# A one-layer decoder trunk with three branches on one core: key tiles 0 and 1 formed together, warm-up products, split operands for sums over partitions, and another order of work at stage ends and in the last rows

## The chip, the cores and the metric

The kernel runs on one core of a Trainium2 chip. TensorE (PE) multiplies matrices, VectorE (DVE) and ScalarE (ACT) do the element-wise work, GpSimd (POOL) issues the stores and some loads, SyncE (SP) issues most loads. Each engine works through its own row of instructions in a fixed order and waits on semaphores of the others. The metric is the device time of the launch in microseconds (us), the median of several runs.

## The reference

One layer on 1024 tokens of width 1024, with a memory of 256 tokens. The functions are cut to their core:

```python
h = rms_norm(x, norm_g)                       # x / sqrt(mean(x^2) + eps) * g
z = einsum('bsd,de->bse', h, w_in)            # 11 column blocks of 1024
u, v, gate_a = gelu(z_u), layer_norm(gelu(z_v)), silu(z_ga)
br_a = gmlp_spatial_gate(u, v, w_s, b_s) * gate_a          # causal within chunks of 128
c = causal_depthwise_conv(z_ba * sigmoid(z_bb), conv_w, conv_b)   # 31 taps
br_b = silu(layer_norm(c, conv_ln_g, conv_ln_b)) * silu(z_gb)
mem_n = rms_norm(mem, mem_norm_g)
att = memory_cross_attention(z_q, mem_n, w_kv)             # 4 heads of 256
br_c = att * silu(z_gc)
proj = einsum('bsnw,nwd->bsnd', [br_a, br_b, br_c], w_branch)
merged = einsum('bsnd,bsnd->bsd', sigmoid(z_merge), proj)
out = rms_norm(x + einsum('bsd,de->bse', merged, w_out), final_norm_g)
```

## The kernel before

All arrays lie in SBUF tiles of 128 partitions. Each large operand is split into two fp32r parts, hi (a cast on ACT) and lo (the difference, on DVE; `split`, lines 74 and 75), and a product is the sum of three: hi by hi, lo by hi, hi by lo. A product named "128x512" in the trace has 512 columns. Products with fp32 operands that are not split show as two records each.

The program goes through these stages, in PE's order (times from the trace):

- Keys (line 231, from 5.86 us): the transposed memory, scaled by its gain (`mhi`, `mlo`, lines 187 and 188), against eight weight tiles e, 24 products of 256 columns each. The sum of squares of memory (`msum`) is added up by DVE (line 130), summed over partitions on PE with a column of ones (line 109 in `mean_rsqrt`), turned into 1/sqrt, and spread over all partitions (`spread`: diagonal matrices `dg` on DVE, line 120, against `ones` on PE, line 121, copied out by ACT, line 122).
- Values of the memory (line 280, from 35 us), eight weight chunks.
- Branch A's v (line 322, from 56 to 149 us): for each half th of the tokens and each half ch of the columns, four weight chunks c, each 24 products of 512 columns into four banks. The first half uses the raw x times its gain (`xg`), and the norm of x, needed by all that comes later, is formed beside it: squares of the eight tiles of x on ACT, adds into `xsum` on DVE (line 130), column sums on PE (line 109), `spread` into `rb`.
- Pairs (line 365, 149 to 928 us): 40 pairs of column tiles of the other blocks, each formed in seven block products instead of eight; x, y, z are its three banks, `op` are split operands, `s1` to `s4` sums of weight quarters, and `u`, `ca`, `cb` intermediate sums on ACT and DVE.
- Branches (line 622, from 929 us): for each branch n in the order 0, 2, 1 and each column tile d, 48 products into `acc`; attention stands between, and the mean (line 764) and the spread of the conv's layer norm between the tiles of n = 2.
- Output projection (line 841, to 1325 us) and the last rows: residual, mean square, 1/sqrt, scaling, store (lines 857 to 875).

A scheduler places instructions in each engine's row when the program is built, by the dependences and by the slots of the pools: a tile takes a slot of its ring (`op`: 6 slots, `raw`: 3, `dg`: 4 in a pool of its own), and a writer stands behind the readers of the slot's last tenant. `keep` fixes the order of loads on SP. Weight chunks come by `wchunk`, a cast of a whole 128x1024 load and its difference.

Of the kernel before, what the change touches and what calls it, by code (L numbers as in the profile page):

```python
# [39 lines left out]
def trunk(ctx, tc, xt, x, memt, wf, wv, wkf, wkv, wbr, wo, wst, bs, cols, fng, out):  # L40
# [110 lines left out]
    A.dma_start(out=col, in_=cols)  # L151

# [32 lines left out]
    for k in range(KT):  # L185
# [3 lines left out]
                               op0=ALU.mult, op1=ALU.subtract)  # L189
    mrb = const.tile([P, M], F32, name="mrb")  # L190
# [27 lines left out]
    for e in range(KT):  # L218
        kv_ahead(e + NAHEAD)
        x_load(e)  # L220
        if e:
            hi, lo = wchunk(None, ahead[e])
        else:
            hi, lo = op((P, 1024), "whi"), op((P, 1024), "wlo")
            for v in (slice(0, H), slice(H, 2 * H)):
                split(ahead[0][:, v], hi[:, v], lo[:, v])
        ps = bank()
        for k in range(KT):
            ks = slice(k * P, (k + 1) * P)
            for j, (w, m) in enumerate(((hi, mhi), (hi, mlo), (lo, mhi))):  # L230
                T.matmul(ps[:, :M], w[:, ks], m[k], start=(k == 0 and j == 0), stop=(k == KT - 1 and j == 2))  # L231
        late.append((e, ps))
# [313 lines left out]
    for p in range(4):  # L546
        for i, (blk, fn, then) in enumerate((
# [20 lines left out]
            pump(PUMP[i])  # L568

# [1 line left out]
    ready = {}  # L571
    order = [(n, d) for n in (0, 2, 1) for d in range(KT)]
    raws = []

# [421 lines left out]
```

## Time and profile before

| what | value |
|---|---|
| median of three runs | 1333.65 us (1333.63 to 1335.38) |
| profiled execution: span from first to last instruction | 1333.8 us |
| PE busy | 1316.5 us (99%) in 6084 records |
| DVE busy | 1079.5 us (81%) |
| ACT busy | 595.3 us (45%) |
| POOL busy | 61.3 us (5%) |
| bytes moved | 179.99 MB |

A timeline row gives the start, the length, the engine, the line, the operation with out<-in by the program's names, and in brackets the idle time before it with what ended it. Products overlap in the pipeline, so the price of one is the distance to the next one's start, not its length.

### The profile page before, as it was taken

What the parts mean: (1) busy time and instruction counts of PE and PEld (TensorE: products, weight loads), DVE (VectorE), ACT (ScalarE), POOL (GpSimd) and SP (SyncE); (2) the same over time, 40 slices, a digit from 0 to 9 for tenths busy, and PEclk for the clock granted to TensorE, in tenths of its full rate; (3) what the DMA queues carried; (4) which work ended last, traced back from release to release, by engine and by line L of the source; (5) the groups of instructions that cost most, each with busy time, mean ns of one, the idle gap of its engine ahead of it and who ended that gap; (6) DMA issues with size and microseconds to landing.
All of it is one profiled execution on the core that took longest, in us unless ns stands there. A gap on an engine that the chain in (4) does not pass through costs nothing.

```text
span 1333.8 us, 16115 instructions
## 1 busy us (share of the span) xinstructions
PE 1316.5 (99%) x6084; PEld 1098.6 (82%) x6084; DVE 1079.5 (81%) x1438; ACT 595.3 (45%) x967; POOL 61.3 (5%) x120
## 2 busy tenths in 40 slices
PE   8999999999999999999999999999999999999997
PEld 7888888888888888888888888887888888888886
DVE  6799759969966998986996996796797486944797
ACT  6757634334444344434434444345544443502256
POOL 0000000000000000000000000001000010000000
PEclk9999999999999999999999999999999999999999
DMA  9634312342222333223333213338555354633323
GB/s 372 248 110 158 135 62 81 111 142 96 103 78 79 121 118 140 88 79 111 111 110 120 95 48 127 127 111 297 188 181 171 112 190 157 228 119 111 142 96 126
DMA packets 60126, 179.99 MB, mean 135 GB/s; under 512 B 5904, under 2 KB 15248, under 8 KB 60048
## 3 DMA queue, kind: packets, MB, share of 16 engines
q1 hardware_dynamic: 44464, 122.96, 27.2%
q0 software_dynamic: 15296, 55.58, 10.9%
q8 instruction: 47, 0.77, 0.2%
q10 hardware_dynamic: 288, 0.42, 0.1%
q14 instruction: 31, 0.25, 0.1%
HBM read 131.75 MB, written 47.19 MB: 134 GB/s over the span
## 4 chain that ended last, share of the span: by engine, by line
PE 95%; DVE 2%; ACT 1%; issue 0%; DMA 0%; SPq 0%; DVEq 0%; ACTq 0%
PE x L365 33%; PE acc L622 19%; PE y L365 16%; PE z L365 8%; PE b L322 6%; PE acc L841 5%; PE b L231 2%; PE acc L660 2%; PE acc L696 2%; PE b L280 1%; PE sp L534 1%; DMA mraw<-in_memt 0%; DVE xsum L130 0%; PE acc L681 0%; ACT y L874 0%
## 5 line engine op out<-in xcount | busy, mean ns | idle before, releaser
L365 PE MATMUL x<-T,op 128*128 128x512 f32 x1440 | 347.5, 390 | 0.7 <-ACT u L404 0.7
L365 PEld LDWEIGHTS x<-T,op 128*128 128x128 f32 x1440 | 269.8, 188 | 57.4 <-ACT u L404 1.1
L74 ACT CAST op<-sum 128x512 fp32r<-128x512 f32 x160 | 99.5, 622 | 132.2 <-PE z L365 56.4
L456 DVE SCALAR_TENSOR_TENSOR conv<-cb,col,conv 128x994 f32<-128x994 f32 (+14 forms) x120 | 151.8, 1265 | 0.5
L75 DVE TENSOR_TENSOR op<-sum,op 128x512 fp32r<-128x512 f32 x160 | 109.4, 686 | 36.0 <-ACT op L74 35.7
L622 PE MATMUL acc<-bhi,whi 128*128 128x512 f32 x384 | 119.7, 393 | 0.9 <-DVE ca L414 0.9
L622 PE MATMUL acc<-bhi,wlo 128*128 128x512 f32 x384 | 119.1, 390 | 0.0
L622 PE MATMUL acc<-blo,whi 128*128 128x512 f32 x384 | 118.7, 390 | 0.0
L365 PE MATMUL x<-B,op 128*128 128x512 f32 x480 | 115.5, 389 | 0.0
L365 PE MATMUL z<-B,op 128*128 128x512 f32 x480 | 115.3, 389 | 0.0
L365 PE MATMUL y<-T,op 128*128 128x512 f32 x480 | 115.3, 389 | 0.0
L365 PE MATMUL y<-B,op 128*128 128x512 f32 x480 | 115.3, 389 | 0.0
L456 DVE SCALAR_TENSOR_TENSOR conv<-ca,col,conv 128x994 f32<-128x994 f32 (+14 forms) x90 | 113.7, 1263 | 0.2
L74 ACT CAST op<-raw 128x512 fp32r<-128x512 f32 x120 | 74.3, 620 | 79.3 <-PE y L365 77.9
L75 DVE TENSOR_TENSOR op<-raw,op 128x512 fp32r<-128x512 f32 x120 | 82.1, 686 | 33.4 <-ACT op L74 33.4
L365 PEld LDWEIGHTS y<-B,op 128*128 128x128 f32 x480 | 90.1, 188 | 18.7
L365 PEld LDWEIGHTS y<-T,op 128*128 128x128 f32 x480 | 90.1, 188 | 18.7
L365 PEld LDWEIGHTS z<-B,op 128*128 128x128 f32 x480 | 90.1, 188 | 18.7
L365 PEld LDWEIGHTS x<-B,op 128*128 128x128 f32 x480 | 90.1, 188 | 18.7
L622 PEld LDWEIGHTS acc<-blo,whi 128*128 128x128 f32 x384 | 72.1, 188 | 15.5 <-DVE blo L75 0.4
L622 PEld LDWEIGHTS acc<-bhi,wlo 128*128 128x128 f32 x384 | 72.1, 188 | 15.0
L622 PEld LDWEIGHTS acc<-bhi,whi 128*128 128x128 f32 x384 | 71.3, 188 | 15.9 <-issue 1.7
(231 smaller groups left out, 1961.2 us busy)
## 6 DMA issues: line engine op xcount, KB each, us to landing
raw<-in_wf SPq DMA_DIRECT2D x80, 512.0 KB, 3.5
raw<-in_wbr SPq DMA_DIRECT2D x24, 512.0 KB, 4.4
gate<-g SPq DMA_DIRECT2D x24, 512.0 KB, 4.2
raw<-in_wv SPq DMA_DIRECT2D x16, 512.0 KB, 3.6
g<-cb POOLq DMA_DIRECT2D x12, 512.0 KB, 3.1
g<-ca POOLq DMA_DIRECT2D x12, 512.0 KB, 2.9
xr<-in_xt SPq DMA_DIRECT2D x8, 512.0 KB, 10.5
kvraw<-in_wkv SPq DMA_DIRECT2D x8, 512.0 KB, 10.7
```

The costliest lines, as they stand in the source:

```text
L74: A.copy(hi, src)
L75: V.tensor_tensor(lo, src, f(hi), ALU.subtract)
L231: T.matmul(ps[:, :M], w[:, ks], m[k], start=(k == 0 and j == 0), stop=(k == KT - 1 and j == 2))
L280: T.matmul(pst[m], a[k][:, ms], w[:, ws], start=(k == 0 and j == 0), stop=(k == KT - 1 and j == 2))
L322: T.matmul(pst[t], q[:, a, ts_], w[:, ws], start=(k == 0 and j == 0), stop=(k == KT - 1 and j == 2))
L365: T.matmul(ps, w[:, a, ks], m[k][:, b, :], start=(start and k == 0 and j == 0), stop=(stop and k == 3 and j == 2), skip_group_check=not start)
L456: V.scalar_tensor_tensor(out=a[:, PAD - j:], in0=g[:, :n], scalar=col[:, cw + j:cw + j + 1], in1=a[:, PAD - j:], op0=ALU.mult, op1=ALU.add)
L534: T.matmul(ps[:, t * P:(t + 1) * P], va[:, 4 * hf + t, :], ws[:, i, :], start=True, stop=True)
L622: T.matmul(ps[:, hf, :], w[:, ks], m[k][:, hf * H:(hf + 1) * H], start=(k == 0 and j == 0), stop=(k == KT - 1 and j == 2))
L660: T.matmul(ps[:, i, :], q[a][:, d, i * P:(i + 1) * P], kk[:, b, d, :], start=(d == 0 and j == 0), stop=(d == 1 and j == 2))
L696: T.matmul(ps[:, d, :], vv[:, a, m, d * P:(d + 1) * P], p2[b][:, m, :], start=(m == 0 and j == 0), stop=(m == MT - 1 and j == 2))
L841: T.matmul(ps[t], a[k][i][:, ts_], w[k][n], start=(start and k == 0 and j == 0), stop=(k == 3 and j == 2), skip_group_check=not start)
```

## The change

Six parts. (1) Ten products of `ones` by `ones` are issued before the first key product; key tiles 0 and 1 are formed side by side, k by k, and the loads of weights and memory alternate in halves. (2) `spread` splits the factor into `rh` and `rl`, builds up to four diagonal matrices by one DVE instruction in a tile of the `op` ring, and spreads by two products of up to 512 columns with an fp32r matrix of ones. (3) In the last pair, the product into z and the start of the branches (`start_branches`) stand between the os3 product and the last one into x. (4) The conv's mean takes a split `csum` and an fp32r `onesd`. (5) The last row tile of the output is formed in two halves of 256 columns. (6) The final norm's small steps are fewer and placed anew, and its last scaling is cut at column 640 instead of 512.

```diff
+        rh = small.tile([P, n], F32R, tag=f"rh{n}", name=nm("rh"))
+        rl = small.tile([P, n], F32R, tag=f"rl{n}", name=nm("rl"))
+        split(r, rh, rl)
+        groups = []
         for i0 in range(0, n, 4):
             w = min(4, n - i0)
+            dg = wpool.tile([P, 2, 4, P], F32R, tag="op", name=nm("dg"), bufs=NOP)
+            for j, v in enumerate((rh, rl)):
+                V.tensor_tensor(dg[:, j, :w, :], ident[:, None, :].broadcast_to([P, w, P]),
+                                f(v)[:, i0:i0 + w, None].broadcast_to([P, w, P]), ALU.mult)
+            groups.append((i0, w, dg))
+        for i0, w, dg in groups:
             ps = mk()
-            for i in range(w):
-                dg = small.tile([P, P], F32, tag="dg", name=nm("dg"), bufs=4)
-                V.tensor_scalar(dg, ident, r[:, i0 + i:i0 + i + 1], None, ALU.mult)
-                T.matmul(ps[:, i * P:(i + 1) * P], ones, dg, start=True, stop=True)
+            for j in range(2):
+                T.matmul(ps[:, :w * P], onesr, dg[:, j, :w, :].rearrange("p a b -> p (a b)"), start=(j == 0),
+                         stop=(j == 1))
             A.copy(dst[:, i0 * P:(i0 + w) * P], ps[:, :w * P])
...
-    onesd = const.tile([P, P], F32, name="onesd")
-    G.memset(onesd, 1.0 / D)
+    onesd = const.tile([P, P], F32R, name="onesd")
+    onesr = const.tile([P, P], F32R, name="onesr")
...
+    ahead.append(slot(s="kvraw"))
+    keep(nc.sync.dma_start(out=ahead[1][:, :H], in_=wkf[1][:, :H]))
     keep(nc.sync.dma_start(out=mraw[0][:, 2:, :], in_=memt[0][:, 2:, :]))
     keep(nc.sync.dma_start(out=ahead[0][:, H:], in_=wkf[0][:, H:]))
-    keep(nc.sync.dma_start(out=mraw[1], in_=memt[1]))
-    kv_ahead(2)
+    keep(nc.sync.dma_start(out=mraw[1][:, :2, :], in_=memt[1][:, :2, :]))
+    keep(nc.sync.dma_start(out=ahead[1][:, H:], in_=wkf[1][:, H:]))
+    keep(nc.sync.dma_start(out=mraw[1][:, 2:, :], in_=memt[1][:, 2:, :]))
+    warm = bank("warm")
+    for _ in range(NWARM):
+        T.matmul(warm[:, :P], ones, ones, start=True, stop=True)
...
+    first = [(op((P, 1024), "whi"), op((P, 1024), "wlo")) for _ in range(2)]
+    for i in range(2):
+        v = slice(i * H, (i + 1) * H)
+        for e in range(2):
+            split(ahead[e][:, v], first[e][0][:, v], first[e][1][:, v])
+            for k in range(4 * i + 2 * e, 4 * i + 2 * e + 2):
+                mem_gain(k)
...
+        if e != 1:
+            group = [(bank(), *(wchunk(None, ahead[e]) if e else first[0]))]
+            if e == 0:
+                group.append((bank(), *first[1]))
+            for k in range(KT):
+                ks = slice(k * P, (k + 1) * P)
+                for ps, hi, lo in group:
+                    for j, (w, m) in enumerate(((hi, mhi), (hi, mlo), (lo, mhi))):
+                        T.matmul(ps[:, :M], w[:, ks], m[k], start=(k == 0 and j == 0),
+                                 stop=(k == KT - 1 and j == 2))
+            for i, g in enumerate(group):
+                late.append((e + i, g[0]))
...
-        o12 = operand(a12)
+        ca, cb = slot(s="ca"), slot(s="cb")
+
+        def second():
+            o12 = operand(a12)
+            prod(z, o12, B[1][0], True, True)
+            V.tensor_tensor(ca[:, :H], z, p1, ALU.add)
+
         V.tensor_tensor(s3, a11, a21, ALU.subtract)
         V.tensor_tensor(s4, a12, s2, ALU.subtract)
-        prod(z, o12, B[1][0], True, True)
-        ca, cb = slot(s="ca"), slot(s="cb")
-        V.tensor_tensor(ca[:, :H], z, p1, ALU.add)
+        if not between:
+            second()
...
         prod(x, os3, T3, False, True)
         u3 = half("u3")
         A.copy(u3, x)
+        if between:
+            second()
+            between()
         V.tensor_tensor(cb[:, H:], y, u3, ALU.add)
...
+    def start_branches():
+        for e in range(NPRE):
+            branch_tile(e, bra[e])
+        for d in range(NRDY):
+            ready[0, d] = weights(0, d)
...
-            pair(blk, p, kept(fn, then))
+            pair(blk, p, kept(fn, then), start_branches if (p, i) == (3, 9) else None)
...
+    csr = wchunk(None, csum)
...
-                T.matmul(ps[:, hf, :], onesd, csum[:, hf * H:(hf + 1) * H], start=True, stop=True)
+                for j in range(2):
+                    T.matmul(ps[:, hf, :], onesd, csr[j][:, hf * H:(hf + 1) * H], start=(j == 0), stop=(j == 1))
...
+            for v in ((slice(0, M), slice(M, H)) if t == fine else (slice(0, H),)):
+                for k in range(4):
+                    for j, (i, n) in enumerate(((0, 0), (1, 0), (0, 1))):
+                        T.matmul(ps[t][:, v], a[k][i][:, ts_], w[k][n][:, v], start=(start and k == 0 and j == 0),
+                                 stop=(k == 3 and j == 2), skip_group_check=not start)
...
+    def yend(i):
+        m, s, y, t, rr = fa[:, i, 1:2], *[fr[:, i, j:j + 1] for j in range(4)]
+        A.activation(out=s, in_=m, func=AF.Sqrt)
+        V.reciprocal(out=y, in_=s)
+        V.scalar_tensor_tensor(out=t, in0=y, scalar=m, in1=y, op0=ALU.mult, op1=ALU.mult)
+        V.tensor_scalar(t, t, -0.5, 1.5, ALU.mult, ALU.add)
+        V.tensor_tensor(rr, y, t, ALU.mult)
+        rows = slice(i * P, (i + 1) * P)
+        if i == 3:
+            w = 640
+            A.activation(out=ys[i][:, w:], in_=ys[i][:, w:], func=AF.Copy, scale=rr)
+            A.dma_start(out=out[rows, w:], in_=ys[i][:, w:])
+            V.tensor_scalar(ys[i][:, :w], ys[i][:, :w], rr, None, ALU.mult)
+            nc.sync.dma_start(out=out[rows, :w], in_=ys[i][:, :w])
...
-    oprod(py, o, w, False)
-    yadd(0, 1, py, 2)
+    oprod(py, o, w, False, 3)
+    for t in range(3):
+        ypart(t, 1, H, 2 * H, py[t], 2)
+        yend(t)
+    ypart(3, 1, H, H + M, py[3][:, :M], 3)
+    ypart(3, 1, H + M, 2 * H, py[3][:, M:], 2, 1)
+    yend(3)
```

What moves in the engines' rows, at three places. In the names, a number tells tiles of one name apart; `x2` is two equal rows; in brackets stands the semaphore waited for.

PE in the first half of branch A's v, before: the end of the second weight chunk (`wlo_165`), the third (`whi_168`), and the column sums of `xsum`.

```order
L322 MATMUL b_136_682<-wlo_165_787,xg_91_487 128x512
L322 MATMUL b_133_679<-whi_168_820,xg_97_498 128x512 [waits Activation_49]
L322 MATMUL b_133_679<-whi_168_820,xg_97_498 128x512
L322 MATMUL b_134_680<-whi_168_820,xg_97_498 128x512 x2
L322 MATMUL b_133_679<-wlo_169_821,xg_97_498 128x512 [waits DVE_49]
L322 MATMUL b_133_679<-whi_168_820,xg_101_519 128x512 x2
L322 MATMUL b_133_679<-wlo_169_821,xg_101_519 128x512
L322 MATMUL b_134_680<-wlo_169_821,xg_97_498 128x512
L109 MATMUL b_147_735<-ones_72,xsum_9_114 128x1 [waits DVE_49]
L109 MATMUL b_147_735<-ones_72,xsum_9_114 128x1 x7
L322 MATMUL b_134_680<-whi_168_820,xg_101_519 128x512 x2
```

The same engine and stage with the change: `whi_140` and `wlo_141` are the first weight chunk, `whi_162` and `wlo_163` the second, `dg` the diagonal matrices.

```order
L348 MATMUL b_138_702<-whi_140_705,xg_78_425 128x512 x2
L348 MATMUL b_138_702<-wlo_141_706,xg_78_425 128x512
L109 MATMUL b_149_755<-ones_72,xsum_14_141 128x1 [waits DVE_49]
L109 MATMUL b_149_755<-ones_72,xsum_14_141 128x1 x7
L129 MATMUL b_159_786<-dg_157_780,onesr_75 128x512 [waits DVE_49] x2
L129 MATMUL b_160_790<-dg_158_783,onesr_75 128x512 [waits DVE_49,Activation_49]
L348 MATMUL b_135_699<-whi_162_796,xg_86_466 128x512 [waits Activation_49]
L348 MATMUL b_135_699<-whi_162_796,xg_86_466 128x512
L129 MATMUL b_160_790<-dg_158_783,onesr_75 128x512 [waits DVE_49]
L348 MATMUL b_136_700<-whi_162_796,xg_86_466 128x512 x2
L348 MATMUL b_137_701<-whi_162_796,xg_86_466 128x512 x2
L348 MATMUL b_135_699<-wlo_163_797,xg_86_466 128x512 [waits DVE_49]
```

The column sums have moved from behind the second chunk and seven products of the third to the place right behind the first chunk, and the spread stands among the first products of the second.

ACT ahead of that place, before: `whi_164` is the cast of the second weight chunk, `vt` the last values of the memory, `xsum` and `sq` the squares of x.

```order
L74 CAST whi_138_685<-raw_137_683 128x1024 [waits DMAHW5_49,DVE_49,PE_49]
L74 CAST whi_164_786<-raw_163_784 128x1024 [waits DMAHW6_49,DVE_49,PE_49]
L287 ACTIVATE vt_126_660<-b_114_592,rs_y_46_257 128x512 [waits PE_49]
L74 CAST v_124_658<-vt_126_660 128x256 [waits Activation_49]
L74 CAST v_125_659<-vt_126_660 128x256
L126 ACTIVATE xsum_9_114<-xr_21_129 128x1024
L287 ACTIVATE vt_127_666<-b_115_593,rs_y_46_257 128x512 [waits PE_49]
L129 ACTIVATE sq_140_714<-xr_34_187 128x1024 [waits DMASW0_49]
```

ACT with the change, at the end of the squares: `whi_162` is the cast of the second weight chunk, `rs_s` the root, `rh` the high part of the factor.

```order
L138 ACTIVATE sq_146_746<-xr_73_389 128x1024
L138 ACTIVATE sq_147_749<-xr_80_430 128x1024 [waits DMASW3_49]
L138 ACTIVATE sq_148_752<-xr_88_471 128x1024
L99 ACTIVATE rs_s_151_766<-ms_150_764 128x8 [waits DVE_49]
L74 CAST rh_155_776<-rs_y_152_767 128x8 [waits DVE_49]
L74 CAST whi_162_796<-raw_161_794 128x1024 [waits DMAHW0_49]
L131 COPY rb_154_775<-b_159_786 128x512 [waits PE_49]
```

The cast of the second chunk stood ahead of vt and the squares, and stands now behind the squares, the root and `rh`.

PE in the last pair, before: the two products into x (`op_1230` is os3, `op_1232` the last), with the product into z long done.

```order
L365 MATMUL x_1220_7199<-T_240_1249,op_1230_7298 128x512 x3
L365 MATMUL x_1220_7199<-T_258_1343,op_1230_7298 128x512 x3
L365 MATMUL x_1220_7199<-T_272_1429,op_1230_7298 128x512 x3
L365 MATMUL x_1220_7199<-T_227_1167,op_1232_7316 128x512 [waits Activation_49]
L365 MATMUL x_1220_7199<-T_227_1167,op_1232_7316 128x512
L365 MATMUL x_1220_7199<-T_227_1167,op_1232_7316 128x512 [waits DVE_49]
L365 MATMUL x_1220_7199<-T_241_1253,op_1232_7316 128x512 x3
```

The same with the change: `op_1227` is os3, `op_1229` the operand of z, `op_1242` that of the last product into x.

```order
L391 MATMUL x_1218_7209<-T_238_1259,op_1227_7292 128x512 x3
L391 MATMUL x_1218_7209<-T_256_1353,op_1227_7292 128x512 x3
L391 MATMUL x_1218_7209<-T_270_1439,op_1227_7292 128x512 x3
L391 MATMUL z_1219_7210<-B_216_1129,op_1229_7309 128x512 x2
L391 MATMUL z_1219_7210<-B_216_1129,op_1229_7309 128x512 [waits DVE_49]
L391 MATMUL z_1219_7210<-B_230_1215,op_1229_7309 128x512 x3
L391 MATMUL z_1219_7210<-B_248_1309,op_1229_7309 128x512 x3
L391 MATMUL z_1219_7210<-B_262_1395,op_1229_7309 128x512 x3
L391 MATMUL x_1218_7209<-T_225_1177,op_1242_7350 128x512 [waits Activation_49]
L391 MATMUL x_1218_7209<-T_225_1177,op_1242_7350 128x512
L391 MATMUL x_1218_7209<-T_225_1177,op_1242_7350 128x512 [waits DVE_49]
```

Twelve products into z have come between the two groups into x.

## Rows read from the trace of the kernel before

**Rows 1.** The page's chain of waits by engine: shares of the span.

```profile
PE 95%; DVE 2%; ACT 1%; issue 0%; DMA 0%; SPq 0%; DVEq 0%; ACTq 0%
```

**Rows 2.** All waits of PE: us in total, times, longest.

```profile
PE b L231 <- ACT mhi L187: 6.2, 2, 5.9
PE acc L622 <- DVE ca L414: 0.9, 1, 0.9
PE x L365 <- ACT u L404: 0.7, 1, 0.7
PE acc L121 <- DVE dg L120: 0.6, 1, 0.6
PE b L322 <- DVE wlo L75: 0.4, 1, 0.4
```

**Rows 3.** Timeline of PE at the start.

```profile
9.44 0.58 PE L231 MATMUL b<-mhi,whi 128*128 128x256 f32 x1 [0.35 <-ACT mhi L187]
...
15.14 0.41 PE L231 MATMUL b<-mhi,whi 128*128 128x256 f32 x1
...
15.35 0.36 PE L231 MATMUL b<-mlo,whi 128*128 128x256 f32 x1
...
15.54 0.28 PE L231 MATMUL b<-mhi,wlo 128*128 128x256 f32 x1
...
15.66 0.28 PE L231 MATMUL b<-mhi,whi 128*128 128x256 f32 x1
...
19.62 0.50 PE L109 MATMUL b<-ones,msum 128*128 128x1 f32 x4
```

**Rows 4.** Timeline of PE in branch A's v, first half.

```profile
57.20 0.62 PE L322 MATMUL b<-whi,xg 128*128 128x512 f32 x2
...
68.08 1.07 PE L322 MATMUL b<-whi,xg 128*128 128x512 f32 x4
...
70.81 1.84 PE L109 MATMUL b<-ones,xsum 128*128 128x1 f32 x16
...
76.02 1.72 PE L121 MATMUL b<-dg,ones 128*128 128x128 f32 x14
```

**Rows 5.** Timeline of DVE at the start.

```profile
11.56 2.36 DVE L75 TENSOR_TENSOR wlo<-kvraw,whi 128x1024 fp32r<-128x1024 f32 x2 [0.45 <-ACT whi L74]
...
13.84 3.60 DVE L130 TENSOR_TENSOR msum<-msum,sq 128x256 f32<-128x256 f32 x7
```

**Rows 6.** Timeline of DVE beside branch A's v.

```profile
61.81 6.54 DVE L130 TENSOR_TENSOR xsum<-xsum,sq 128x1024 f32<-128x1024 f32 x5
...
68.27 1.22 DVE L75 TENSOR_TENSOR wlo<-raw,whi 128x1024 fp32r<-128x1024 f32 x1
...
69.40 1.22 DVE L130 TENSOR_TENSOR xsum<-xsum,sq 128x1024 f32<-128x1024 f32 x1
```

**Rows 7.** Timeline of DVE at the conv's norm.

```profile
1121.29 0.17 DVE L111 TENSOR_SCALAR ms<-acc 128x8 f32<-128x8 f32 x1 [3.63 <-PE acc L109]
...
1122.78 0.88 DVE L120 TENSOR_SCALAR dg<-ident,rs_y 128x128 f32<-128x128 f32 x4
```

**Rows 8.** Windows at the end: length, busy by engine, clock, DMA share, GB/s.

```profile
1326.00:1330.00 4.00, 0.00 (x0) 0.00 (x0) 3.15 (x15) 2.66 (x7) 0.00 (x0) 0.95 0.53 215
1330.00:1334.00 4.00, 0.00 (x0) 0.00 (x0) 0.00 (x0) 0.15 (x1) 0.00 (x0) 0.50 0.46 178
```

**Rows 9.** Timeline of PE at the conv's mean.

```profile
1069.12 1.02 PE L764 MATMUL acc<-csum,onesd 128*128 128x512 f32 x2
...
1072.22 0.63 PE L622 MATMUL acc<-blo,whi 128*128 128x512 f32 x2
```

**Rows 10.** Timeline of PE at the conv norm's spread.

```profile
1126.69 1.05 PE L121 MATMUL acc<-dg,ones 128*128 128x128 f32 x8
```

**Rows 11.** Timeline of PE and ACT's queue at the end.

```profile
1325.04 0.39 PE L841 MATMUL acc<-olo,op 128*128 128x512 f32 x1
...
1330.18 0.35 ACTq L870 DMA_DIRECT2D out<-y  x1
```

More of the change, by code (lines that the diff above doesn't have):

```diff
@@ L151, in trunk @@
     A.dma_start(out=col, in_=cols)
+    A.copy(onesr, ones)
+    A.mul(onesd, ones, 1.0 / D)
     def c1(base, k):
@@ L184, in trunk, with mem_gain @@
     mlo = [mlo2[k // 4][:, k % 4, :] for k in range(KT)]
-    for k in range(KT):
+    def mem_gain(k):
         src = mraw[k // 4][:, k % 4, :]
@@ L220, in trunk @@
         x_load(e)
[L221 to L232, printed above, removed]
+        if e != 1:
[10 more added lines that the diff above has]
+                late.append((e + i, g[0]))
         if e == 0:
@@ L371, in operand, with pair @@
         return o
-    def pair(blk, p, consume):
+    def pair(blk, p, consume, between=None):
         r0, r1 = raw_load(wf[blk, 2 * p]), raw_load(wf[blk, 2 * p + 1])
@@ L542, in ugate, with fetch, weights, branch_tile @@
         return then
+    ready = {}
+    order = [(n, d) for n in (0, 2, 1) for d in range(KT)]
+    raws = []
+    def fetch(upto):
+        for i in range(len(raws), min(upto, len(order))):
+            raws.append(raw_load(wbr[order[i]], True))
+    def weights(n, d):
+        i = order.index((n, d))
+        fetch(i + 1)
+        return wchunk(None, raws[i])
+    bhi, blo = [None] * KT, [None] * KT
+    def branch_tile(e, val):
+        bhi[e] = slot(F32R, s="bhi")
+        blo[e] = slot(F32R, s="blo")
+        split(val, bhi[e], blo[e])
+    def start_branches():
[3 more added lines that the diff above has]
+            ready[0, d] = weights(0, d)
     bra = {}
@@ L568, in trunk @@
             pump(PUMP[i])
-    ready = {}
-    order = [(n, d) for n in (0, 2, 1) for d in range(KT)]
-    raws = []
-    def fetch(upto):
-        for i in range(len(raws), min(upto, len(order))):
-            raws.append(raw_load(wbr[order[i]], True))
-    def weights(n, d):
-        i = order.index((n, d))
-        fetch(i + 1)
-        return wchunk(None, raws[i])
-    bhi, blo = [None] * KT, [None] * KT
-    def branch_tile(e, val):
-        bhi[e] = slot(F32R, s="bhi")
-        blo[e] = slot(F32R, s="blo")
-        split(val, bhi[e], blo[e])
     kv = {}
@@ L594, in kv_load @@
         kv[hd] = (load(kdram[hd], F32R, (P, 2, 2, M), "k"), load(vdram[hd], F32R, (P, 2, MT, HD), "v"))
-    for d in range(NRDY):
-        ready[0, d] = weights(0, d)
     pend.pop(0)()
-    for e in range(NPRE):
-        branch_tile(e, bra[e])
     kv_load(0)
@@ new lines, in yadd, with ypart @@
+            ypart(4 * r + t, c, c * H, (c + 1) * H, ps[t], last)
+            if last == 2:
+                yend(4 * r + t)
+    def ypart(i, c, x0, x1, p, last, n=0):
+        v = ys[i][:, x0:x1]
+        V.tensor_tensor(v, v, p, ALU.add)
+        if last:
+            q = c + n
+            sq = wpool.tile([P, 1024], F32, tag="raw", name=nm("fsq"), bufs=NRAW)
+            A.activation(out=sq[:, :x1 - x0], in_=v, func=AF.Square, accum_out=fs[:, i, q:q + 1])
+            V.tensor_tensor(v, v, fg[:, x0:x1], ALU.mult)
+            if last == 1:
+                V.tensor_scalar(fa[:, i, 0:1], fs[:, i, q:q + 1], 1.0 / D, RMS_EPS, ALU.mult, ALU.add)
+            elif last == 2:
+                V.tensor_scalar(fa[:, i, 1:2], fs[:, i, q:q + 1], 1.0 / D, fa[:, i, 0:1], ALU.mult, ALU.add)
+            else:
+                V.tensor_scalar(fa[:, i, 0:1], fs[:, i, q:q + 1], 1.0 / D, fa[:, i, 0:1], ALU.mult, ALU.add)
@@ L939 @@
 PUMPA = 8
+NWARM = 10
 PUMP = (6, 4, 6, 3, 6, 8, 6, 6, 5, 7)
```

38 lines of the change are left out of this document (11 added, 27 removed).

## The prediction

> **What bounds the kernel now.** I read the chain of waits first: it lies on PE, the tensor engine, for 95% of the span [rows 1]. So an edit counts only by what it adds to or takes from PE's row of work: products fewer, products cheaper, or idle time of PE. The waits of PE come next [rows 2]: 8.8 us in all, of which 6.2 are the start, and four single waits of 0.4 to 0.9 us. There is little to win: the idle time, and the few products that are not part of the big matrices. There is much more to lose, for DVE, ACT and the loads are all hidden today, and anything that makes PE wait for them is paid in full. The last view is the timeline of PE, ACT and DVE around each place that the diff touches. The profiled execution took 1333.8 us, 0.15 above the median of the three runs (1333.65); I add my terms to the median.
>
> Prices on PE, by distances between starts: a 128x256 product 0.21 us at the lower clock level, 1.2 GHz (15.14 to 15.35), and 0.12 at the upper, 2.4 GHz (15.54 to 15.66) [rows 3]. A 128x512 product costs 0.227 (48 products from 57.20 to 68.08); an fp32 128x128 one is two records, fourteen of which took 1.72 with the tail, so about 0.11 each; the column sums of xsum are sixteen records in 1.84 [rows 4].
>
> **1. Start (memory blocks and the first two key tiles).** The ten warm-up products stand before any data is there, so they cost nothing as long as they end before the first operand, at 5.9 [rows 2]: 20 records at twice 0.11 make 4.4 us, and the work before them is one fill of ones. Two key tiles from the same memory tiles leave PE twice as much to do per landed block, which fills the gap before 9.44, and the faster clock comes earlier than 15.35 [rows 3]. What ends last then is not PE. The next things in PE's row are tile 2 and the column sums of line 109, which need the seven adds of msum on DVE. Those take 3.60 us behind the low part of tile 2 [rows 5], whose weights come after the same 2 MB as before, so they end at about 17.4. The sums began at 19.62 [rows 3] and will begin at 17.4: -2.2 us. Bounds: 0 if the clock comes no earlier; -5.0 if the adds didn't hold (72 products of 0.12 from 5.9 end at 14.6). The memory gain's own spread (mrb) becomes two products of 256 columns for two fp32 ones, 0.24 for 0.45: -0.2.
>
> **2. The norm of x, the term that decides.** Before, the column sums of xsum stood in PE's row behind all of weight chunk 1 and seven products of chunk 2. In the new order they stand right behind chunk 0. The reason is on ACT: the new dg tiles take slots of the same ring as the weights' hi and lo parts, and the cast of chunk 1 moved from ahead of vt to behind rs_s and rh. PE finishes chunk 0's 24 products at 57.20 + 24 x 0.227 = 62.65. The sum isn't there: ACT's squares and the DVE adds behind them are untouched by the diff. Five adds run from 61.81 to 68.35; the last one, which now doesn't have a low part ahead of it, runs 68.27 to 69.5 [rows 6]. As before, PE starts 0.2 behind it: 69.7. So PE waits 7.0 us with chunks 1 to 3 queued behind the sums; their weights' loads wait in turn for the slots that the casts free, but stand landed by then.
>
> Then 1.84 us of sums, and a second wait: the chain mean, root, four DVE steps, 1.46 us (as from 1121.29 to the first dg at 1122.78 in the conv norm, where nothing stood in between [rows 7]) to 73.0; rh and rl 0.2 each (tiny DVE steps are 0.17 [rows 7]), four dg halves of 512 columns at 0.6 (two low parts of 1024 took 2.36 [rows 5]), and the low part of chunk 1, 1.2, behind them: 77.1. In that time PE does four spread products and six of chunk 1. From there 66 of the 96 products of this half are left: 66 x 0.227 = 15.0, end at 92.1. Before, the end was at 57.20 + 21.8 + 1.7 (sums) + 1.8 (sixteen spread records) + 0.75 (the wait of 0.4 [rows 2] and, as an estimate, as much for the refills beside it) = 83.25. So +8.9 us with the clock held, and the spread's saving of 0.9 and the removed wait are in that.
>
> The clock is the second part. After the last product of the program the granted clock was still 0.95 over 1326 to 1330 and 0.50 from 1330 to 1334 [rows 8]: it fell within the pause that follows the last product. A wait of 7.0 us is nearly as long as that whole pause of 8. The sums then cost up to 1.7 more and the chain behind them comes as much later; and the products after 77.1 run at 0.43 (twice 0.21 [rows 3]) until the clock is back. At the start that took 9.5 us, from 5.9 to 15.35: 22 products, 4.4 us lost. Bounds for the clock: 0 to 7.0 (1.7 + 0.9 in the pieces of chunk 1 + 4.4). I take 1.7 + 2.2 = 3.9, since the products after 77.1 stand close together, while those of the start had the gap before 9.44 among them. Sum of part 2: +12.8.
>
> The Trainium skill ("TensorE: Matmul & The Clock Gate", "Architectural detail") says that only weight loads are pulled ahead of products in flight, products keep their order, and ACT and DVE are strict queues. By that rule nothing of chunk 1 can slip past the sums; the trace agrees, since PE's row went in the listed order at the wait before 922 too. The same page of the Trainium skill ("HAM oscillation — how this bites in real kernels") holds that a long enough pause between products brings the lower clock back, which this trace shows only at its end, with 0.50; by it the first rival below would be out.
>
> **3. Pairs and their end.** Inside the pairs the lists move by a row or two on DVE, which has room (no wait of PE is on DVE there): 0. In the last pair the z product, which doesn't need the newest sum, goes between the os3 product and the last x product, and the first branch weights and operands are cast there. That covers the 0.7 wait on u with its refill: -0.95. The 0.9 wait of the first branch product on ca stays, since ca's add still follows the last y product. Bounds: -1.9 if that goes too, +1.0 if the casts put in there hold the next operands.
>
> **4. Conv mean.** Two fp32 products of 512 columns become four split ones. From 1069.12 to 1072.22 PE had six plain products (1.36) and the fp32 ones [rows 9], so 1.74 for these; four at 0.227 are 0.91: -0.8, and about 0.2 of small refills: -1.0. The split of csum, a cast on ACT and a low part of 1.2 on DVE, is ahead of that, in a stretch where PE waits for neither [rows 2]. Bounds -1.5 to +1.2, the latter if PE waits for that low part.
>
> **5. Conv norm's spread.** Sixteen fp32 records (1.8) and the wait of 0.6 on the gate add with its refill [rows 2, 10] become four products of 0.227: -1.7. The four dg halves are ready at about 1125.9 (chain to 1122.78 [rows 7], rh and rl, four by 0.6), before PE's spread slot at 1126.69. Bounds -2.0 to +0.5, the latter if the low part of the next weights comes late behind them.
>
> **6. Last rows.** Half of the last row tile's epilogue runs beside its second half of products; these cost 24 x 0.12 for 12 x 0.227, +0.16. From the last product's start to the last issue were 5.1 us [rows 11]; the add, square and gain in it become 256 columns wide for 512, and two tiny DVE steps of 0.17 go: an estimate of -0.55. Sum -0.4. Bounds -1.0 to +0.5.
>
> **Sum.** -2.2 - 0.2 + 12.8 - 0.95 - 1.0 - 1.7 - 0.4 = +6.35 on 1333.65: 1340.0 us.
>
> **Rivals.**
> *The wait is there, the clock stays* (the six products and the sums between the two waits keep it up): +12.8 becomes +8.9, 1336.1 us. For it: the page's clock row never falls before the end. Against it: no wait in this program but the start's exceeds 0.9 us, so it never had cause. Chance 0.14.
> *A long cold stretch*: as slow as at the start, the whole 7.0: +15.9 instead of 12.8, 1343.1 us. For it: the only rise in this trace took 9.5 us. Against: those were broken by a gap. Chance 0.12.
> *The sums don't hold PE* (the change doesn't do on the chip what the order says, or chunk 1's products go ahead while the adds run): then part 2 is -0.9 for the spread and -0.76 for the old wait, and the sum is 1333.65 - 6.45 - 1.65 = 1325.55 us, faster. It decides as long as the two waits together stay under 5.4 us (6.45 + 1.65 - 2.7) and the clock holds. Against it are the list of ACT, which holds chunk 1's cast back as well, and the seven adds of 1.3 us; for it, only that the row before ran through this place with a wait of 0.4. Chance 0.08.
>
> **How the numbers follow.** The forecast has 0.66, with 1337 to 1343 by the bounds of its own terms. What this kernel's measurement can tell from no change is about 0.2%, 2.7 us: up to 1336.3. Slower by more: 0.63 of the forecast's 0.66, all of the cold rival's 0.12, a little of the first rival's (0.03): 0.78. Same: 0.09 of the first rival's, 0.02 of the forecast's: 0.11. Faster: 0.08, and 0.03 for the case that start, pair end and tail all come out at their good bounds under a held clock: 0.11. The range for 8 in 10 runs from 1333 (the first rival with better edges) to 1344.5 (the cold rival, with the start's gain at 1 us).
>
> **What would show it.** Right: in the profile after, PE's longest wait past the start is for xsum's last add, 6 to 8 us, at about 60; a second one of 1 to 4 us for dg and the low part of chunk 1; the granted clock of 60 to 80 below 1.00; line 109's first sums at about 17.4; no wait on u at the pair's end; the spread of the conv norm in four products without a wait. Wrong: PE passing from chunk 0 to chunk 1 with less than 5 us of idle time, or a chain that has shares of DVE and ACT no larger than now.

## The result and the profile after

The changed kernel takes **1349.97 us** (median of four runs, 1349.7 to 1350.13); the kernel before, 1333.76 (four runs, 1333.63 to 1335.38). The ratio is 1.0118, with a 95% interval of 1.0106 to 1.0131: 1.2% slower. The forecast was 1340.0 with a range of 1333 to 1344.5. Its direction and its largest term came out; the time lies 5.5 us above the range. The profiled execution of one run below, the changed kernel with the pair's end as before, took 4254 us and is left out of that run's median.

The chain of waits after, by engine, against [rows 1]:

```profile
PE 93%; DVE 3%; ACT 2%; issue 1%; DMA 1%; SPq 0%; POOL 0%; DVEq 0%; POOLq 0%; ACTq 0%
```

DVE, ACT and DMA have 6% where they had 3%: PE now waits for others. For whom, the waits of PE say (us in total, times, longest), against [rows 2]:

```profile
PE b L109 <- DVE xsum L139: 6.9, 1, 6.9
PE y L391 <- DVE cb L439: 3.2, 1, 3.2
PE b L129 <- DVE dg L123: 2.6, 1, 2.6
PE acc L658 <- DVE blo L75: 1.9, 3, 1.4
```

The first and third rows are the forecast ones: the last add of xsum, then dg. The second and fourth stand in no term of the forecast: the last y product of the last pair waits for cb, and the first tile of branch n = 1 for its operands' low parts. The waits of 0.7 on u and of 0.6 on dg in the conv norm are gone.

The places of branch A's v, in PE's timeline after (start, duration, instruction), against [rows 4]:

```profile
60.81 0.39 PE L348 MATMUL b<-wlo,xg 128*128 128x512 f32 x1
68.12 3.57 PE L109 MATMUL b<-ones,xsum 128*128 128x1 f32 x16 [6.92 <-DVE xsum L139]
74.27 2.06 PE L129 MATMUL b<-dg,onesr 128*128 128x512 f32 x3 [2.58 <-DVE dg L123]
76.13 1.05 PE L348 MATMUL b<-whi,xg 128*128 128x512 f32 x2
...
77.41 1.91 PE L348 MATMUL b<-whi,xg 128*128 128x512 f32 x4
```

The sixteen column sums take 3.57 us for 1.84, and the products from 76.13 to 80.40, ten of them, are 0.427 apart for 0.227. Windows of the same stretch (length, busy us of PE, PE's weight loads, DVE, ACT and POOL, granted clock, DMA share, GB/s) show why:

```profile
64.00:68.00 4.00, 0.00 (x0) 0.00 (x0) 3.69 (x4) 0.65 (x1) 0.00 (x0) 0.50 0.00 1
68.00:72.00 4.00, 3.57 (x16) 3.49 (x16) 0.23 (x2) 0.07 (x1) 0.00 (x0) 0.50 0.01 4
72.00:76.00 4.00, 1.73 (x3) 1.04 (x4) 3.43 (x11) 1.58 (x4) 0.00 (x0) 0.50 0.00 0
76.00:80.00 4.00, 4.00 (x11) 3.03 (x11) 3.55 (x5) 3.28 (x5) 0.00 (x0) 0.50 0.38 121
80.00:90.00 10.00, 10.00 (x45) 8.23 (x44) 8.87 (x13) 2.89 (x4) 0.00 (x0) 0.98 0.54 161
```

The clock falls to 1.2 GHz within the first wait and is back only after 80, behind the stretch of close products. The Trainium skill ("TensorE: Matmul & The Clock Gate", "HAM oscillation — how this bites in real kernels") says that a long enough pause between products brings the lower clock back; this trace agrees, with a granted clock of 0.50 from 64 to 80.

By comparing when PE starts the same product in both traces, the shift can be followed along the program. This is my own reckoning, after minus before, in us, each taken where the shift has settled:

| place in PE's row | shift there | change since the line above | forecast |
|---|---|---|---|
| start of branch A's v | -1.61 | -1.61 | -2.4 |
| end of that stage | +11.24 | +12.85 | +12.8 |
| start of the branches (pairs' end) | +13.90 | +2.66 | -0.95 |
| after the conv mean | +13.26 | -0.64 | -1.0 |
| after the conv norm's spread | +11.48 | -1.78 | -1.7 |
| within the first tile of branch n = 1 | +14.37 | +2.89 | 0 |
| start of the output projection | +14.38 | 0.0 | 0 |
| end of the span | +14.23 | -0.15 | -0.4 |

Two lines come out far from the forecast, the pairs' end and the first tile of branch n = 1, and both have their cause on DVE. At the last pair's end, in DVE's timeline:

```profile
934.76 3.50 DVE L75 TENSOR_TENSOR blo<-bra,bhi 128x1024 fp32r<-128x1024 f32 x3 [0.26 <-ACT bhi L74]
938.17 0.68 DVE L439 TENSOR_TENSOR cb<-y,u 128x512 f32<-128x512 f32 x1
```

and in PE's:

```profile
932.90 2.88 PE L391 MATMUL x<-T,op 128*128 128x512 f32 x12
939.00 2.98 PE L391 MATMUL y<-B,op 128*128 128x512 f32 x12 [3.22 <-DVE cb L439]
```

The x products end at about 935.8, and cb's add frees the accumulator that y needs. But the three low parts of the branch operands, 3.5 us, now stand ahead of that add on DVE; it runs at 938.17, and PE goes on at 939.00. The shift falls from +11.38 to +10.42 where the wait on u was, and rises to +13.90 at this wait.

The other place, DVE's timeline ahead of branch n = 1 after:

```profile
1170.90 1.23 DVE L792 TENSOR_TENSOR cm<-cm,sgb 128x1024 f32<-128x1024 f32 x1 [2.83 <-DMA sgb<-sgb]
1172.04 2.35 DVE L75 TENSOR_TENSOR wlo<-raw,whi 128x1024 fp32r<-128x1024 f32 x2
1174.31 2.35 DVE L75 TENSOR_TENSOR blo<-cm,bhi 128x1024 fp32r<-128x1024 f32 x2
```

and of before:

```profile
1157.39 1.23 DVE L755 TENSOR_TENSOR cm<-cm,sgb 128x1024 f32<-128x1024 f32 x1 [2.06 <-DMA sgb<-sgb]
1158.53 1.22 DVE L75 TENSOR_TENSOR wlo<-raw,whi 128x1024 fp32r<-128x1024 f32 x1
1159.67 5.76 DVE L75 TENSOR_TENSOR blo<-cm,bhi 128x1024 fp32r<-128x1024 f32 x5
```

With the shift of 11.5 the first low part would stand at 1159.67 + 11.5 = 1171.2; it stands at 1174.31, 3.1 later. 1.1 of that is the second wlo ahead of it, 2.0 the last sgb load's landing. That load, on POOL's queue, is issued beside the next weights' load on SP's:

```profile
1163.91 0.96 SPq L82 DMA_DIRECT2D raw<-in_wbr  x1
...
1164.04 0.54 POOL L146 DMA_DIRECT2D sgb<-sgb  x1 [1.16 <-PE acc L658]
```

and needs 6.9 us to its add (before: issued at 1152.23, 1.2 after the weights' load, 5.2 to its add).

### The profile page after: what moved, and what is told of

The parts are those of the page before. It is cut to its first block, busy times and chain, and to the rows that moved or that the text cites. A ratio compares the mean times of both kernels' runs of the same rounds, so it can differ in the third digit from the quotient of the medians.

```text
span 1348.0 us, 16122 instructions
## 1 busy us (share of the span) xinstructions
PE 1321.9 (98%) x6090; PEld 1102.6 (82%) x6090; DVE 1083.5 (80%) x1431; ACT 595.8 (44%) x976; POOL 60.6 (4%) x119
## 4 chain that ended last, share of the span: by engine, by line
PE 93%; DVE 3%; ACT 2%; issue 1%; DMA 1%; SPq 0%; POOL 0%; DVEq 0%; POOLq 0%; ACTq 0%
PE x L391 32%; PE acc L658 16%; PE y L391 16%; PE z L391 8%; PE b L348 6%; PE acc L880 5%; PE b L255 2%; PE acc L696 2%; PE acc L732 2%; PE b L306 1%; PE sp L568 1%; DVE xsum L139 1%; DMA sgb<-sgb 1%; DVE blo L75 1%; PE acc L717 0%
```

## The experiments

Theory: the dg tiles of the new spread, as tiles of the op ring, hold back the weights' casts behind them (norm of x, branch n = 1), and the moved casts hold cb's add. Rivals: the column sums were late for another cause (order of ACT, x's squares); the clock, not the waits, is most of it; the other edits (warm-up, two tiles at once) have a price that the rows hide. Ratios are against the kernel before on the same chip; its median there was 1333.8 to 1335.3, so times from different chips are compared by what they lie above it.

**The dg tiles out of the op ring** (label a_slot), the rest as changed:

```
-            dg = wpool.tile([P, 2, 4, P], F32R, tag="op", name=nm("dg"), bufs=NOP)
+            dg = slot(F32R, (P, 2, 4, P), "dg")
```

> The kernel after, with one edit: the diagonal matrices of the spread take a slot of the large 36-slot ring instead of the 6-slot ring of the split operands. Theory A (the ring is the cause): with the slots of the split operands free, the sums of xsum stand again behind weight chunk 1 and part of chunk 2, the wait of 6.9 us on the last add and the one of 2.6 us for dg go, with the cold stretch behind them (13.7 us in all by the shift of PE's row), and so do the waits on blo in the branches (2.6 us), since there too the diagonal matrices held slots that the next weights needed: 1333.7 us. Rival B (the ring matters in branch A's v alone; the waits on blo come from the conv's split mean): 1336.3. Rival C (the sums wait because PE is earlier at them, whatever the ring): 1350, with a wait of 6 to 7 us on xsum still there.

Measured: 1338.29 us (9 runs), ratio 1.0022 (1.0011 to 1.0032). The wait on xsum is gone and that on blo too; the whole stage of branch A's v goes from +12.85 to -1.05. So the ring is the cause of both. It came out 4.6 above what I expected. 1.4 of that is the kernel before, which took 1335.2 on this chip and not 1333.8. In the profiled execution, two places pay more than I had counted. The larger is a new wait at the memory gain's spread, in PE's timeline:

```profile
27.65 0.72 PE L129 MATMUL b<-dg,onesr 128*128 128x256 f32 x2 [2.66 <-DVE dg L123]
...
29.28 0.42 PE L255 MATMUL b<-mhi,whi 128*128 128x256 f32 x1
29.49 0.42 PE L255 MATMUL b<-mlo,whi 128*128 128x256 f32 x1
```

and in DVE's:

```profile
26.03 1.23 DVE L75 TENSOR_TENSOR wlo<-kvraw,whi 128x1024 fp32r<-128x1024 f32 x1 [1.11 <-ACT whi L74]
27.17 0.42 DVE L123 TENSOR_TENSOR dg<-ident,rh 128x256 fp32r<-128x256 f32 x1
```

With dg in the large ring two more weight tiles are split ahead of it. PE waits 2.7, and its products are 0.21 apart from 28.6 to about 32. The end of the keys moved from -1.6 to +3.4. The other place is the wait on cb, which is as long as in the changed kernel, but is followed here by a granted clock of 0.70 from 928 to 932, so that the twelve y products take 4.57 for 2.98:

```profile
929.62 4.57 PE L391 MATMUL y<-B,op 128*128 128x512 f32 x12 [3.22 <-DVE cb L439]
```

This execution took 1339.04, 0.8 above the median, so not every one need pay at both.

**cb's add ahead of the casts** (a_cb), the rest as changed:

```
+        V.tensor_tensor(cb[:, H:], y, u3, ALU.add)
+        if between:
             between()
-        V.tensor_tensor(cb[:, H:], y, u3, ALU.add)
```

> The kernel after, with one edit: in the last pair the add into cb stands ahead of the start of the branches instead of behind it. Theory A (the 3.2 us wait of the last y product is for this one add, which stands on DVE behind three low parts of branch operands): the wait goes, -3.4 us, 1346.6. Rival B (the DVE row in front of the first branch product is only shifted: the low parts come later and PE waits for them or for ca instead): 1349 to 1350.

Measured: 1347.83 (4 runs), ratio 1.0095 (1.008 to 1.011): between the theory and the rival. The wait on cb is gone and the stage comes to -0.84 for +2.66, near the -0.95 of the forecast. What it gains, 3.5 in that stage, is partly paid later:

```profile
PE acc L659 <- DVE blo L75: 2.7, 2, 2.2
...
PE acc L659 <- DVE ca L449: 1.1, 1, 1.1
```

The branch operands are now cast behind cb: branch n = 0 loses 1.6 by the shift, with the waits on ca and blo, and the waits on blo come to 2.7 in all for 1.9. The longer of them, 2.2 in branch n = 1, is followed by a granted clock of 0.62 from 1174 to 1178, and that place costs 4.1 for 2.9. The cause of the 3.2 is shown; neither of these two places for the moved casts is free.

**Both of them** (best1):

> Both edits, the other ring for the diagonal matrices and the add into cb first. If both theories A hold, the terms add: 1350.0 - 16.3 - 3.4 = 1330.3 us, below the kernel before (1333.8). If either rival holds, 1333 or more.

Measured: 1334.68 (10 runs), ratio 0.9998 (0.9988 to 1.0007): as before. The wait of 2.7 for the memory gain's dg is there as in the first of these experiments, and takes what the other edits give.

**Products in the wait** (a_fill): the changed kernel with 28 products of 512 columns, whose results nobody reads, between chunk 0 and the column sums.

```
+                        fl = bank("fl")
+                        for _ in range(28):
+                            T.matmul(fl, xg[0][:, 0, :P], hi[:, :H], start=True, stop=True)
```

> The kernel after, with 28 products of 512 columns added into a bank of their own, which nobody reads, between chunk 0 and the sums of xsum (28 x 0.227 = 6.4 us of work in a wait of 6.9 us). It tells the wait from the clock. Theory A (part of the loss is the lower clock: sums at 0.213 instead of 0.112, ten products at 0.427 instead of 0.227, spread products slow): the granted clock stays 1.00 up to the sums, these take 1.8 us instead of 3.4, and the run is 3 to 4 us faster than the kernel after, about 1346.5. Rival B (the clock falls anyway in the second wait of 2.6 us, or the low clock is hidden by DVE's chain): 1348 to 1350.

Measured: 1346.01 (4 runs), ratio 1.0085 (1.0069 to 1.01). The windows there:

```profile
64.00:68.00 4.00, 3.42 (x19) 2.61 (x17) 3.09 (x3) 0.00 (x0) 0.00 (x0) 1.00 0.00 0
68.00:72.00 4.00, 1.33 (x13) 1.28 (x12) 1.98 (x9) 1.35 (x3) 0.00 (x0) 0.94 0.00 0
72.00:76.00 4.00, 4.00 (x9) 2.82 (x10) 3.55 (x6) 2.27 (x4) 0.00 (x0) 0.50 0.05 14
```

With the first wait filled the clock holds through it, and the sums cost 1.95:

```profile
67.36 1.95 PE L109 MATMUL b<-ones,xsum 128*128 128x1 f32 x16 [0.58 <-DVE xsum L139]
71.97 1.97 PE L129 MATMUL b<-dg,onesr 128*128 128x512 f32 x3 [2.67 <-ACT whi L74]
```

But in the second wait, of 2.7, the clock fell all the same, to 0.50 from 72 to 76. The stage is +11.36 for +12.85. So filling only the first wait gets 1.5 of the clock's cost back; the wait itself stays. The time is near the expected one, but not by the expected term alone: of the 4.3 by which the span is shorter than the changed kernel's (1343.7 for 1348.0), 1.5 is this stage, 0.8 the start, and 2.0 the wait on blo, which is only 0.2 here. The rows tell why: the last sgb load is issued at 1161.78, 0.8 ahead of the weights' load, and its add starts 4.9 after it without a wait. The second wlo stands ahead of the low parts here too, and the place costs 0.9. In the changed kernel and the two other variants that have this wait (a_cb and b_spread, 2.2 and 2.1 of it in one piece), the two loads are issued within 0.3 of each other, and the add starts 6.9, 7.6 and 7.5 after.

**Before with the new spread alone** (b_spread), dg in the op ring:

```
+            dg = wpool.tile([P, 2, 4, P], F32R, tag="op", name=nm("dg"), bufs=NOP)
...
-                dg = small.tile([P, P], F32, tag="dg", name=nm("dg"), bufs=4)
```

> The kernel before with one part of the change alone: the new spread, its diagonal matrices in the ring of the split operands. If that part carries the loss, PE's row shifts by +12.9 us in branch A's v (7 us waiting for the last add of xsum, 2 to 3 for dg, the rest the lower clock), -1.5 at the conv norm's spread, and +2.6 where PE waits for blo behind it: +14 us on the kernel before, about 1349 beside 1335. Rival (it needs the earlier start or the split mean beside it): less than +8.

Measured: 1349.4 (4 runs), ratio 1.0109 (1.0093 to 1.0124). Its waits of PE:

```profile
PE b L109 <- DVE xsum L139: 6.9, 1, 6.9
...
PE b L129 <- DVE dg L123: 2.6, 1, 2.6
PE acc L633 <- DVE blo L75: 2.1, 1, 2.1
```

One edit out of the whole change gives both places: +12.5 at the norm of x and +4.0 in branch n = 1, with -1.77 at the conv norm's spread. The wait on blo is followed here by a granted clock of 0.57 from 1176 to 1180, which it isn't in the changed kernel. That its time is nearly that of the whole change is chance, since the rest of the change by the table above (-1.61, +2.66, -0.64 and -0.15) comes to about nothing. The rivals that put the late sums down to the other edits fall.

**The wide spreads' dg in the large ring, the memory gain's in the op ring**, with cb first (best3), and with the pair's end as before the change (best2):

```
+            dg = (slot(F32R, (P, 2, 4, P), "dg") if n > MT else
+                  wpool.tile([P, 2, 4, P], F32R, tag="op", name=nm("dg"), bufs=NOP))
```

> The kernel after with the diagonal matrices of the two eight-wide spreads in the large ring, those of the memory gain's in the ring of the split operands as in the kernel after, and the add into cb first. The run with all of them in the large ring had a wait of 2.7 us for dg at the memory gain and lost some 4 us there with the clock; theory A says that this goes and nothing else moves: 4 us under that run (1334.7), so about 1331 beside 1335 of the kernel before. Rival: the wait for dg there has another cause and stays: 1334 to 1335.

Measured: 1330.69 (9 runs), ratio 0.9973 (0.9964 to 0.9983).

> As the run before it in this list, but the last pair and the start of the branches in the old order. With the z product moved PE saves the wait on u (0.7 us and refill) and pays 1.2 us for low parts of branch operands that come later; so the old order is as good or better: 0 to 0.7 us less, 1330.3 to 1331. Rival (the new order with the add first is a gain): 0.8 us more.

Measured: **1329.85** (5 runs), ratio 0.9969 (0.9956 to 0.9981): 0.3% faster than the kernel before. That the old order of the pair's end is better than the new one with cb first isn't shown: the intervals of the two runs overlap. Its longest waits past the first operand:

```profile
PE acc L663 <- DVE ca L449: 0.9, 1, 0.9
PE x L392 <- ACT u L436: 0.7, 1, 0.7
PE b L109 <- DVE msum L140: 0.6, 1, 0.6
```

Its shift against the kernel before is -2.2 at the end of the keys, -1.1 in branch A's v, -0.6 at the conv mean and -1.8 at the conv norm: the change's parts, without the two that cost. In branch A's v the rival in which the sums don't hold PE had -0.9 for the spread and -0.76 for the old wait; the wait of 0.4 on wlo is still there. Of the -2.2, up to 1.5 may belong to the execution and not to the change, as the second profile of the kernel before shows below. The window from 64 to 70 has a clock of 1.00 in this execution.

**The same without warm-up products** (best2_w0): `NWARM = 10` becomes `NWARM = 0`.

> As the run before it, without the ten warm-up products. Theory A (they bring the faster clock earlier): the rise from 0.21 to 0.12 us a product comes later than with them (8 to 12 us so far), the column sums of the memory start late, and the median is 1 to 3 us longer. Rival B (the clock rises when it does whatever stands before the data; the key stage is held by the adds of msum anyway): within 0.5 us.

Measured: 1329.91 (5 runs), ratio 0.9967 (0.9955 to 0.998), so no difference that can be told. PE at the start without them:

```profile
8.75 0.37 PE L256 MATMUL b<-mlo,whi 128*128 128x256 f32 x1
8.96 0.28 PE L256 MATMUL b<-mhi,wlo 128*128 128x256 f32 x1
...
16.82 0.58 PE L109 MATMUL b<-ones,msum 128*128 128x1 f32 x4 [0.71 <-DVE msum L140]
```

and with them:

```profile
6.67 0.35 PE L256 MATMUL b<-mhi,whi 128*128 128x256 f32 x1
6.87 0.28 PE L256 MATMUL b<-mlo,whi 128*128 128x256 f32 x1
...
17.32 0.61 PE L109 MATMUL b<-ones,msum 128*128 128x1 f32 x4 [0.61 <-DVE msum L140]
```

The products get to their faster pace 2 us later, but PE waits 0.6 to 0.7 for msum either way: as the forecast had it, what ends last there is not PE. So the warm-up gives nothing here that can be told. What gain the start has would then come from the order of the loads and the two tiles; no run takes these out alone.

**z moved and cb first, only weights cast there** (best4), on the version with the wide spreads' dg in the large ring:

> As the run with the last pair in the old order (1329.85), but with the z product moved as in the change, the add into cb first, the first branch weights cast there, and the first branch operands cast where they stood before the change. Theory A: the wait on u goes (0.7 us and refill, as in the run with the add first) and the low parts of the branch operands come no later than before, so PE doesn't wait for blo: -0.85, 1329.0. Rival (casting the weights alone already makes the operands late): 1329.8 to 1330.5.

Measured: 1330.4 (7 runs), ratio 0.9972 (0.9961 to 0.9983), which can't be told from the 0.9969 of the old order; I expected 1329.0. The wait on u is gone (-0.96 by the shift), but that on ca is 1.1 for 0.9, and branch n = 0 loses another 0.8. Rearranging the pair's end brings nothing that these runs can tell.

**The changed kernel with the pair's end as before** (a_nob):

```
-            pair(blk, p, kept(fn, then), start_branches if (p, i) == (3, 9) else None)
+            pair(blk, p, kept(fn, then), None)
...
+    for d in range(NRDY):
+        ready[0, d] = weights(0, d)
     pend.pop(0)()
+    for e in range(NPRE):
+        branch_tile(e, bra[e])
```

> The kernel after with the last pair and the start of the branches alone in the old order. Theory A (that part is a loss as the change has it): the wait of 3.2 us for cb goes and the one of 0.7 on u is back: PE's row gains 2.6 us there, 1347.4 beside 1350.0. Rival (the part is neutral, the wait only shows what was late anyway): 1349.5 to 1350.

Measured: 1346.0 (3 runs), ratio 1.0083 (1.0069 to 1.0098). That is 10.7 above the kernel before on its chip, where the whole change is 16.2 above: 5.5 less, for 2.66 by the table above. The ends of the two intervals leave anything from 1 to 8, so that this part is a loss is shown, and its size isn't. Its rows are not compared here.

**The kernel before once more** (b_again), for a second profile:

> The kernel before, unchanged, for a second profile of its start. The profiled run of it had a span 1.7 us above the median of the timed ones. Theory A: the rest is the moment when the clock rises at the start (15.35 us in that profile); here it comes at another moment, and the span differs by the share of cold products. Rival: the spans differ elsewhere (loads, last rows).

Measured: 1335.62, span 1333.9 (the first: 1333.8). The same span comes about by other places. Its faster pace starts at 9.9 us instead of 15.5, and the keys end 1.5 earlier:

```profile
9.87 0.28 PE L231 MATMUL b<-mhi,wlo 128*128 128x256 f32 x1
9.99 0.28 PE L231 MATMUL b<-mhi,whi 128*128 128x256 f32 x1
```

But from 72 to 76 it has

```profile
72.00:76.00 4.00, 4.00 (x14) 3.14 (x14) 2.24 (x10) 0.00 (x0) 0.00 (x0) 0.69 0.68 240
```

where the first profile of before has

```profile
72.00:76.00 4.00, 4.00 (x21) 3.42 (x22) 2.97 (x11) 0.21 (x1) 0.00 (x0) 1.00 0.79 206
```

which costs it 1.6. The spans of the kernel before lie from 1331.4 to 1335.5 over all its runs, and the timed figure is the span + 1.7 in every run of every kernel here.

## Why the prediction was wrong

**Norm of x: right, in mechanism and size.** Forecast: 7.0 us of wait, sums up to 1.7 dearer, a second wait of 1 to 4, a clock below 1.00 from 60 to 80, +12.8. Measured: 6.9, 1.7 dearer (3.57 for 1.84), 2.6, 0.50, and +12.85. The clock's share was put at 3.9; by rows it is 1.7 in the sums and about 2.0 in ten products at 0.427 for 0.227, 3.7. That the products lose half of what the start lost was a choice of the forecast, so the closeness of that term is partly luck. The rivals on this place (clock stays; long cold stretch; sums don't hold PE) fell. The cause, dg in the op ring, is shown from both sides: alone it makes the wait, elsewhere it doesn't.

**Pairs and their end: wrong, +2.66 for -0.95; 3.6 of the miss.** The step said that the z product and the casts put in there cover the wait on u, and they did: that wait went, for -0.96. It counted them as cover on PE's side and didn't write down what stands behind them on DVE. That is three low parts of 1.17, and then cb's add, for which the next twelve products wait. My bad bound, "+1.0 if the casts put in there hold the next operands", looked at the operands and not at the accumulator. DVE's rows after show it: 3 x 1.17 = 3.5 us of low parts, a wait of 3.2, and 3.5 in PE's shift. Putting cb first removes the wait, and the kernel with the old order there lies 10.7 above the kernel before, for 16.2.

**Conv norm's spread: right in itself (-1.8 for -1.7), wrong about what it sets off: +2.9 for 0.** (Its own terms put the dg halves at 1125.6 and not 1125.9, which changes nothing.) I priced the four dg products and the possible delay of the next weights, +0.5 at most, and went no further down the queue. In the op ring dg's tiles delay the weights' casts, so that two wlo for one stand ahead of the first blo (1.1), and the weights' load comes to stand beside the last sgb load, whose add comes 2.0 later. With dg in the large ring neither is there; with the products in the wait the second wlo is there and the meeting isn't, and the place costs 0.9. The same edit had been seen through at the norm of x and not at its second use. How the ring's tiles lead to that very meeting of the two loads, step by step, wasn't followed.

**Base: 1.7 of the miss.** I read 1333.8 as the profiled execution's time; it is its span. The timed figure is 1.7 above the span, so that execution is the run of 1335.38, the slowest of the three, 1.7 above their median. The terms came from it and were added to the median. On its own time the same sum is 1341.7.

**Start: -1.61 for -2.4, and not shown to be the change's.** The first sums of line 109 stand at 17.92 for 19.62, forecast 17.4. But the second profile of the kernel before has them at 18.15 and its keys end 1.5 earlier with no change at all, with a clock that rose earlier. So the 15.35 from which the term was read belongs to one execution, and what the change gives here stays open. In this execution of the changed kernel products ran at 0.21 again from about 8.9 to 12.16, and so PE came to the sums behind the adds:

```profile
17.92 0.57 PE L109 MATMUL b<-ones,msum 128*128 128x1 f32 x4
```

There is no wait on msum here. The faster version above has it, with its sums at 17.32 and -2.2: there what ends last is not PE, as the forecast said.

**Conv mean** -0.6 for -1.0; **last rows** -0.15 for -0.4. From the last product's start to the last issue it was 4.71 for 5.14, so the half of the last tile's epilogue that runs beside products gives 0.4:

```profile
1339.68 0.28 PE L880 MATMUL acc<-olo,op 128*128 128x256 f32 x1
...
1344.39 0.35 ACTq L925 DMA_DIRECT2D out<-y  x1
```

Together: 3.6 (pairs' end) + 2.9 (branch n = 1) + 1.7 (base) + 0.8 (start) + 0.4 (conv mean) + 0.2 (last rows) - 0.1 (spread) = 9.5, of the 9.97 between 1340.0 and 1349.97; 0.3 is the median above the profiled run of 1349.7. The range failed since it held no case in which moved work on DVE costs PE more than 1.2 at a place outside branch A's v; the two that did are 6.5 together.

## What to carry to other kernels

A tile's ring is part of the order: a small tile put into the ring of a busy stream can take that stream's place. Here it did so at two of the helper's three uses, and at the third the other ring was the dear one, so each call has to be followed on its own, past the instructions moved to the loads that their slots start. Where work is put into a gap on one engine, write down what is queued behind it on the engines that do it, accumulators to be freed included, before calling it covered. And add the terms to the time of the execution that they were read from, its span plus what lies around it, before going over to the median; a term read from the moment at which the clock rises in one profile may not be there in the next.

## What the runs showed of the hardware that was not expected

After one wait of 2.66 us (25.0 to 27.65, in the first experiment) the products ran at their full pace of 0.12 until about 28.5 and only then at 0.21, until about 32: there the clock's fall came behind the pause. In the wait of 6.9 us it fell within it.

Waits of like length at one place did not cost the same. The one of 3.2 us on cb left the granted clock at 1.00 in the changed kernel (935 to 943) and was followed by 0.70 from 928 to 932 in the first experiment, which made it 1.6 dearer. The waits on blo of 2.2 and 2.1 us (a_cb, b_spread) were followed by 0.62 and 0.57 over 4 us.

The rise differs between executions of the same program: the kernel before got its faster pace at 15.5 us in one and at 9.9 in the other. In the second a wait of 0.4 with 1.8 us of one-column products was followed by a granted clock of 0.69 from 72 to 76, in the first it stayed at 1.00. The same is seen between two versions that are alike there: 0.78 from 72 to 76 in best3, 1.00 in best2. So single profiles of this kernel differ by 1 to 2 us at such a place.

Where the sgb load and a load of weights were issued within 0.3 us of each other on two queues, the sgb load's add came 6.9 to 7.6 us behind its issue. With the sgb load 0.8 us ahead it came 4.9 behind, and in the kernel before, with the weights 1.2 us ahead, 5.2.
